# Hybrid mLSTM / attention block: the gate columns join the last v projection, and one v projection becomes 512 columns wide

## The chip, the cores and the metric

The kernel runs on one core of a Trainium2 chip. The metric is the device time of one launch in microseconds (us); lower is better. TensorE is called PE here, its weight loads PEld, VectorE DVE, ScalarE ACT, GpSimd POOL, and the queue that starts DMAs SP.

## What is computed

One layer of a decoder trunk with two token mixers side by side, on 512 tokens of width 1024, in fp32 (cut):

```python
h = rmsnorm(x, norm_g[l]) * (1.0 + scale[:, None]) + shift[:, None]
proj = h @ w_in[l]                       # 1024 -> 14344 columns
(qm, km, vm, om, zm, im, fm, qa, ka, va, za, gm, ga) = jnp.split(proj, split_idx, axis=-1)
...
im = im + b_if[l, :M_HEADS]              # input gate, 4 columns
fm = fm + b_if[l, M_HEADS:]              # forget gate, 4 columns
hm = mlstm_chunkwise(qm, km, vm, im, fm) # 4 heads
...
ha = diff_attention(qa, ka, va, lam, rel_bias)   # 8 heads, v of a head has 128 columns
ya = ha @ w_proj_a[l]
y = sigmoid(gm) * ym + sigmoid(ga) * ya
x = x + gate[:, None] * (y @ w_out[l])
return rmsnorm(x, final_g)
```

Of the 14344 columns only 8 are the gates `im` and `fm`; the attention's `va` has 1024, 256 for each pair of heads.

## The kernel before

Every fp32 product is made of three matmuls on split operands. A value is the sum of a rounded half `hi` and a rest `lo`, and `mm3` (lines 132 to 141) adds hi*hi, hi*lo and lo*hi into one PSUM bank. The normed input is held as `h_hi` and `h_lo` (8 blocks of 128 rows by 512 tokens) for the whole kernel.

Weights come in granules of 128x1024 fp32 (512 KB). `split_granule` (148 to 154) starts the DMA into a `raw` buffer, ACT casts it to `whi` (line 99) and DVE subtracts to get `wlo` (line 117). Each of the three has three buffers, so a granule's cast waits until PE is through with the granule three earlier. The table `_granules` (40 to 57) lays the columns of `w_in` out in the order of use: "F" granules hold q, k, v and z of the first pair of heads for one block of 128 rows; "B" 128 columns for all rows; "A" 256 columns for half of the rows; "W" 512 columns for a quarter of the rows.

The program runs in three parts.

1. **First pair** (lines 602 to 663). For each of 8 row blocks PE makes q, k, v and z of heads 0 and 1 while DVE and ACT still norm the input. Then `evac_qa`, `evac_ka`, `evac_v` and `silu2` empty the eight PSUM banks.
2. **Attention** (665 to 707). The heads are generators; `tick` (158) moves each one a step forward after every projection, so that their short matmuls lie between long projections. First `if_gates` (524 to 595) is started: it makes a granule of its own out of the 8 gate columns (a POOL memset, four DMAs, a cast, a subtraction), multiplies it in 16 matmuls (line 539), adds the bias, and in the steps after that works out log sigmoid, the running sum and maximum over the tokens, and writes two rows per head to `me_d` in DRAM; the mLSTM reads them back (lines 781, 782). Then for each pair `p` of 1 to 3: q, k, a merge gate, v (`proj_v`, 368 to 375, twice 4 row blocks), a merge gate, then the same q and k for the second head, and z. `proj_v` computes v with the tokens on the partitions: the stationary operand is a 128x128 block of h, the moving one 256 columns of weights, four token blocks in two banks.
3. **mLSTM, projections, output** (890 to 1013), four heads with `proj_w` (379 to 391) for v, 512 columns wide, one bank for each of the four token blocks.

PSUM has 8 banks: 4 of the pool `acc` for projections and 4 of `core` for the heads. A new tile takes the bank that was given up first. Each engine works through its queue in order; a scheduler sets that order when the program is built, from the order of the code and the priorities.

Of the kernel before, what the change touches and what calls it, by code (L numbers as in the profile page):

```python
# [9 lines left out]
F32 = mybir.dt.float32  # L10
# [53 lines left out]
@with_exitstack  # L64
def hybrid_block_kernel(ctx: ExitStack, tc: tile.TileContext, xT, x, c, wada2, wada, win, wif, wpm, wpa, wout,
                        small, lamv, bif, relb, onehot, fing, out):
# [75 lines left out]

    def load_granule(src):
        raw = stg.tile([P, D], F32, tag="raw", name=nm("raw"))
        nc.sync.dma_start(raw, src)
        return raw

    def split_granule(src):
        raw = load_granule(src)
        hi = stg.tile([P, D], F32R, tag="whi", name=nm("whi"))  # L150
        lo = stg.tile([P, D], F32R, tag="wlo", name=nm("wlo"))
        with tc.high_priority():
            split(hi, lo, raw, eng="act")
        return hi, lo
# [22 lines left out]
    lam4 = sb.tile([P, 384], F32, tag="bt", bufs=3, name="lam4")  # L177
    bift = const.tile([MH, 2], F32, name="bift")
    oneh = sb.tile([32, RL], F32, tag="bt", bufs=3, name="oneh")
# [49 lines left out]

    csl = sb.tile([P, D], F32, tag="v", bufs=2, name="csl")  # L230
    csl_done = []
# [127 lines left out]
    def evac_v(pss):  # L359
        v = sb.tile([P, 2, NT, 256], F32R, tag="v", bufs=2, name=nm("v"))  # L360
        vh, vl = v[:, 0], v[:, 1]
        for i in range(2):
            split(vh[:, 2 * i:2 * i + 2, :].rearrange("p a b -> p (a b)"),
                  vl[:, 2 * i:2 * i + 2, :].rearrange("p a b -> p (a b)"), pss[i])
        return vh, vl


    def proj_v(col, half, pss):
        hi, lo = split_granule(win[GIDX[("A", col, half)]])
        for kk in range(4):  # L370
            wsl = slice(kk * 256, kk * 256 + 256)
            mm_v(pss, half * 4 + kk, (hi[:, wsl], lo[:, wsl]))
        v = evac_v(pss) if half else None
        tick()
        return v

    def proj_w(col, quarter, pss, v):
        hi, lo = split_granule(win[GIDX[("W", col, quarter)]])  # L380
        for t in range(NT):
            for kk in range(2):
                k = quarter * 2 + kk
                tsl, wsl = slice(t * P, (t + 1) * P), slice(kk * S, (kk + 1) * S)
                mm3(pss[t], (h_hi[:, k, tsl], h_lo[:, k, tsl]), (hi[:, wsl], lo[:, wsl]), k == 0, k == NK - 1)
            if quarter == 3:
                if t % 2 == 0:
                    w = sb.tile([P, 2, 2, S], F32R, tag="v", bufs=2, name=nm("v"))
# [43 lines left out]
    ha = [None] * AH  # L432
    za = [None] * AH
    va = [None] * AH

    def hp_tiles():
# [5 lines left out]
    def attn_head(hd, q, k):  # L442
# [3 lines left out]
        bt = bias_tile(hd)  # L446
        vs = slice((hd % 2) * P, (hd % 2) * P + P)
        pt = sb.tile([P, 2, 1280], F32, tag="p", bufs=PB, name=nm("pt"))
# [46 lines left out]
        for kb in range(NT):  # L495
            c0 = min(kb, 2) * P
            a = slice(KOFF[kb], KOFF[kb] + S - c0)
            mm3(ps[:, c0:S], (va[hd][0][:, kb, vs], va[hd][1][:, kb, vs]), (ah[:, a], al[:, a]),
                kb == 0, kb == NT - 1, head=True)
# [22 lines left out]
    me_d = dram.tile([MH, 2 * S], F32, name="me_d")  # L522

    def if_gates():

        wraw = stg.tile([P, D], F32, tag="raw", name="wraw_if")
        nc.gpsimd.memset(wraw, 0.0)
        wr3 = wraw.rearrange("p (k n) -> p k n", n=P)
        for o in (0, 64):
            nc.sync.dma_start(wr3[:, :, o:o + MH], wif[:, :, MH:2 * MH])  # L530
            nc.sync.dma_start(wr3[:, :, o + 32:o + 32 + MH], wif[:, :, 0:MH])
        wih = stg.tile([P, D], F32R, tag="whi", name="wih")
        nc.scalar.copy(wih, wraw)
        wm = wih.rearrange("p (k n) -> p k n", n=P)
        nc.vector.tensor_tensor(wm[:, :, 64:128], wr3[:, :, 64:128], wm[:, :, 64:128].bitcast(F32), ALU.subtract)
        ps = acc_ps()
# [4 lines left out]
        g_i = sb.tile([P, S], F32, tag="z", bufs=8, name="g_i")[0:MH, :]  # L541
        g_p = sb.tile([P, S], F32, tag="z", bufs=8, name="g_p")[0:MH, :]
        for g, o, col in ((g_p, 0, 1), (g_i, 32, 0)):
            nc.scalar.activation(g, ps[o:o + MH, :], AF.Identity, bias=bift[:, col:col + 1])
            nc.vector.tensor_tensor(g, ps[o + 64:o + 64 + MH, :], g, ALU.add)
        yield
        for _ in range(2):
            yield

        ps = core_ps()  # L550
        for t in range(NT):
# [50 lines left out]
    for k in range(NK):  # L602
# [36 lines left out]
        if k == 1:  # L639
            nc.sync.dma_start(lam4[:, 0:256], lamv)  # L640
            nc.sync.dma_start(bift, bif)
        if k in (5, 6):
# [17 lines left out]
    q1, k1 = evac_qa(fq[1]), evac_ka(fk[1])  # L660
    va[0] = va[1] = evac_v(fv)
# [203 lines left out]
    def out_weights(k):  # L865
# [4 lines left out]
        elif k < 7:  # L870
            tag, bufs = {3: ("v", 2), 4: ("p", PB), 5: ("p", PB), 6: ("sw", 1)}[k]
            w2 = sb.tile([P, 2, D], F32R, tag=tag, bufs=bufs, name=nm("wo"))
# [17 lines left out]
    for h in range(MH):  # L890
# [11 lines left out]
        if h == 0:  # L902
            while None in ha:
                tick()
# [33 lines left out]

    gf = sb.tile([P, 2, D], F32, tag="v", bufs=2, name="gf")
    gate_b, fg = gf[:, 0, :], gf[:, 1, :]  # L940
# [143 lines left out]
```

## Time and profile before

| what | us |
|---|---|
| median of 3 runs | 925.57 (925.35 to 926.0) |
| profiled execution, own time | 924.88 |
| its span, first to last instruction | 923.1 |
| PE busy | 908.9 (98%) |
| DVE busy | 601.7 (65%) |
| ACT busy | 454.9 (49%) |
| POOL busy | 24.3 (3%) |

A matmul's busy time in the profile overlaps with the next one's, so a busy share of 98% does not say how much work PE has; the distance from one start to the next does. A row of the timeline gives start, duration, engine, line, operation, operands (partitions x elements) and a count; in square brackets how long the engine had been idle before it, and what released it.

### The profile page before, as it was taken

What the parts mean: (1) busy time and instruction counts of PE and PEld (TensorE: products, weight loads), DVE (VectorE), ACT (ScalarE), POOL (GpSimd) and SP (SyncE); (2) the same over time, 40 slices, a digit from 0 to 9 for tenths busy, and PEclk for the clock granted to TensorE, in tenths of its full rate; (3) what the DMA queues carried; (4) which work ended last, traced back from release to release, by engine and by line L of the source; (5) the groups of instructions that cost most, each with busy time, mean ns of one, the idle gap of its engine ahead of it and who ended that gap; (6) DMA issues with size and microseconds to landing.
All of it is one profiled execution on the core that took longest, in us unless ns stands there. A gap on an engine that the chain in (4) does not pass through costs nothing.

```text
span 923.1 us, 11500 instructions
## 1 busy us (share of the span) xinstructions
PE 908.9 (98%) x4351; PEld 762.5 (83%) x4351; DVE 601.7 (65%) x975; ACT 454.9 (49%) x741; POOL 24.3 (3%) x56
## 2 busy tenths in 40 slices
PE   6999999999999999999999999999999999999997
PEld 3888987988888888888888888888888888888886
DVE  7967788878666565435558544586554877638944
ACT  7546887766677554222354533454233553236422
POOL 0001010000001000000000000000000000000000
PEclk8999999999999999999999999999999999999999
DMA  9863414333422352432223223223132224336421
GB/s 343 336 186 119 131 65 138 126 137 126 149 84 100 117 169 100 151 137 89 87 76 111 93 72 93 89 96 110 69 114 69 92 99 152 137 114 223 142 80 57
DMA packets 40656, 114.90 MB, mean 124 GB/s; under 512 B 8289, under 2 KB 8553, under 8 KB 39578
## 3 DMA queue, kind: packets, MB, share of 16 engines
q1 hardware_dynamic: 40010, 113.11, 35.6%
q10 hardware_dynamic: 592, 1.07, 0.4%
q8 instruction: 34, 0.56, 0.2%
q14 instruction: 20, 0.16, 0.1%
HBM read 106.78 MB, written 10.00 MB: 127 GB/s over the span
## 4 chain that ended last, share of the span: by engine, by line
PE 92%; DVE 3%; DMA 2%; ACT 2%; issue 1%; SPq 0%; ACTq 0%
PE acc L134 26%; PE acc L135 26%; PE acc L136 26%; PE core L134 3%; PE core L135 3%; PE core L136 3%; PE core L459 1%; PE core L460 1%; PE core L489 1%; DVE wlo L117 1%; DMA relt<-in_relb_dram 1%; PE core L237 1%; DMA xt<-in_xT_dram 1%; ACT whi L99 0%; DMA ga<-gt_d 0%
## 5 line engine op out<-in xcount | busy, mean ns | idle before, releaser
L134 PE MATMUL acc<-h_hi,whi 128*128 128x512 f32 x688 | 269.1, 391 | 0.5 <-DVE qk L427 0.5
L117 DVE TENSOR_TENSOR wlo<-raw,whi 128x1024 fp32r<-128x1024 f32 x129 | 157.8, 1223 | 167.7 <-ACT whi L99 163.5
L99 ACT CAST whi<-raw 128x1024 fp32r<-128x1024 f32 x129 | 135.5, 1050 | 245.5 <-PE acc L135 175.9
L135 PE MATMUL acc<-h_lo,whi 128*128 128x512 f32 x656 | 255.8, 390 | 0.0
L136 PE MATMUL acc<-h_hi,wlo 128*128 128x512 f32 x656 | 255.5, 389 | 0.0
L134 PEld LDWEIGHTS acc<-h_hi,whi 128*128 128x128 f32 x688 | 129.4, 188 | 26.6 <-PE acc L539 0.8
L136 PEld LDWEIGHTS acc<-h_hi,wlo 128*128 128x128 f32 x656 | 123.2, 188 | 25.9
L135 PEld LDWEIGHTS acc<-h_lo,whi 128*128 128x128 f32 x656 | 123.3, 188 | 23.9
L134 PE MATMUL acc<-whi,h_hi 128*128 128x512 f32 (+1 forms) x224 | 77.1, 344 | 0.1
L136 PE MATMUL acc<-whi,h_lo 128*128 128x512 f32 (+1 forms) x224 | 77.0, 344 | 0.0
L135 PE MATMUL acc<-wlo,h_hi 128*128 128x512 f32 (+1 forms) x224 | 76.9, 343 | 0.0
L134 PE MATMUL acc<-hh,whi 128*128 128x512 f32 x192 | 74.7, 389 | 0.0
L135 PE MATMUL acc<-hl,whi 128*128 128x512 f32 x192 | 74.7, 389 | 0.0
L136 PE MATMUL acc<-hh,wlo 128*128 128x512 f32 x192 | 74.7, 389 | 0.0
L134 PEld LDWEIGHTS acc<-whi,h_hi 128*128 128x128 f32 x224 | 42.4, 189 | 5.5 <-ACT tmp L741 0.5
L135 PEld LDWEIGHTS acc<-wlo,h_hi 128*128 128x128 f32 x224 | 42.4, 189 | 5.0
L136 PEld LDWEIGHTS acc<-whi,h_lo 128*128 128x128 f32 x224 | 42.4, 189 | 5.0
L464 ACT ACTIVATE pt<-pt,mn 128x128 f32<-128x128 f32 (+3 forms) x64 | 35.5, 557 | 17.6 <-DVE mn L462 17.4
L136 PEld LDWEIGHTS acc<-hh,wlo 128*128 128x128 f32 x192 | 36.1, 188 | 7.5
L135 PEld LDWEIGHTS acc<-hl,whi 128*128 128x128 f32 x192 | 36.1, 188 | 7.4
L134 PEld LDWEIGHTS acc<-hh,whi 128*128 128x128 f32 x192 | 36.1, 188 | 7.4
L462 DVE CUSTOM_DVE_ANT_0 pt<-core,bt 128x128 f32<-128x128 f32 (+3 forms) x64 | 29.5, 486 | 14.7 <-PE core L460 14.3
(277 smaller groups left out, 1360.2 us busy)
## 6 DMA issues: line engine op xcount, KB each, us to landing
raw<-in_win_dram SPq DMA_DIRECT2D x112, 512.0 KB, 3.3
wa<-in_wada_dram SPq DMA_DIRECT2D x8, 1024.0 KB, 7.1
raw<-in_wpm_dram SPq DMA_DIRECT2D x16, 512.0 KB, 3.2
raw<-in_wada_dram SPq DMA_DIRECT2D x8, 512.0 KB, 3.2
raw<-in_wpa_dram SPq DMA_DIRECT2D x8, 512.0 KB, 3.4
raw<-in_wout_dram SPq DMA_DIRECT2D x8, 512.0 KB, 3.3
gt_d<-tmp SPq DMA_DIRECT2D x12, 256.0 KB, 2.2
toe_d<-rev_d SPq DMA_DIRECT2D x8, 320.0 KB, 6.2
```

Of the source, the lines that this page charges most:

```text
L99: recent["act"] = nc.scalar.copy(dst, src)
L117: recent["dve"] = nc.vector.tensor_tensor(lo, src, hi.bitcast(F32), ALU.subtract)
L134: a = nc.tensor.matmul(ps, lhs[0], rhs[0], start=start, stop=False)
L135: b = nc.tensor.matmul(ps, lhs[l[0]], rhs[l[1]], start=False, stop=False)
L136: c = nc.tensor.matmul(ps, lhs[r[0]], rhs[r[1]], start=False, stop=stop)
L237: a = nc.tensor.matmul(idle, ones_r, ones_w, start=True, stop=True)
L459: inorder(nc.tensor.matmul(ps, q[m][:, qs], kh[m][:, 0:wn], start=True, stop=False))
L460: inorder(nc.tensor.matmul(ps, q[m][:, qs], kl[m][:, 0:wn], start=False, stop=True))
L462: nc.vector.tensor_tensor_reduce(pp, ps[:, 0:w], bt[:, S - w:S], 1.0, BIG, ALU.add, ALU.min, mn[:, qb, m:m + 1])
L464: nc.scalar.activation(pp, pp, AF.Exp, scale=-1.0, bias=mn[:, qb, m:m + 1], accum_out=ls[:, qb, m:m + 1])
L489: inorder(nc.tensor.transpose(ps[:, n:n + P], pt[:, 0, o:o + P], ident))
```

## The change

The granule form "A" and `proj_v` are gone. v of pairs 1 and 2 is made in one `proj_w` of 512 columns, in pair 1's place; nothing stands in pair 2's place. v of pair 3 is made by a new `proj_g` from two granules of 128x1056 (`wvg`): 256 columns of v and the 8 gate columns side by side, 264 columns for each of four banks. The first part of `if_gates` (memset, DMAs, split, 16 matmuls, bias) is gone; the generator now starts after pair 3's `proj_g` and takes the gates from an SBUF tile `gates`, tokens on the partitions. So the forget gates need no transposition to begin with, and the input gates need four (new). The pool tag `v` has 3 buffers instead of 2, and the SBUF area kept for DMA descriptors shrinks from 8192 to 2048 bytes. The mLSTM's first head waits in the program text for `gates_done`.

```diff
     for p in range(1, 4):
         g += [("B", C_QA + 256 * p), ("B", C_KA + 256 * p)]
-        g += [("A", C_VA + 256 * p, 0), ("A", C_VA + 256 * p, 1)]
+        if p == 1:
+            g += [("W", C_VA + 256, i) for i in range(4)]
...
-    def proj_v(col, half, pss):
-        hi, lo = split_granule(win[GIDX[("A", col, half)]])
-        for kk in range(4):
-            wsl = slice(kk * 256, kk * 256 + 256)
-            mm_v(pss, half * 4 + kk, (hi[:, wsl], lo[:, wsl]))
-        v = evac_v(pss) if half else None
+    def proj_g(half, pss):
+        hi, lo = split_granule(wvg[half], 4 * VG)
+        if half:
+            w = sb.tile([P, 2, NT, 256], F32R, tag="v", bufs=VB, name=nm("v"))
+        for t in range(NT):
+            for kk in range(4):
+                k = half * 4 + kk
+                tsl, wsl = slice(t * P, (t + 1) * P), slice(kk * VG, (kk + 1) * VG)
+                mm3(pss[t][:, 0:VG], (h_hi[:, k, tsl], h_lo[:, k, tsl]), (hi[:, wsl], lo[:, wsl]), k == 0, k == NK - 1)
+            if half:
+                split(w[:, 0, t, :], w[:, 1, t, :], pss[t][:, 0:256])
+                nc.vector.tensor_tensor(gates[:, t, :], pss[t][:, 256:VG], bift, ALU.add)
         tick()
...
     def if_gates():
-        wraw = stg.tile([P, D], F32, tag="raw", name="wraw_if")
...
-        for k in range(NK):
-            for i, hx in enumerate((h_hi, h_lo)):
-                nc.tensor.matmul(ps, wih[:, k * P:(k + 1) * P], hx[:, k, :], start=(k == 0 and i == 0),
-                                 stop=(k == NK - 1 and i == 1))
...
-            pin(nc.tensor.transpose(ps[:, t * MH:(t + 1) * MH], g_p[:, t * P:(t + 1) * P], ident[0:MH, 0:MH]), "pe")
...
-        nc.vector.tensor_copy(f, ps[:, 0:NT * MH])
+        nc.vector.tensor_copy(f.rearrange("p (a b) -> p a b", b=MH), gates[:, :, MH:2 * MH])
...
         nc.scalar.copy(g_p, ps[0:MH, :])
         yield
+        ps = core_ps()
+        for t in range(NT):
+            pin(nc.tensor.transpose(ps[0:MH, t * P:(t + 1) * P], gates[:, t, 0:MH], ident), "pe")
+        nc.scalar.copy(g_i, ps[0:MH, :])
+        yield
...
-    gens.append(if_gates())
-    tick()
     gens.append(attn_head(0, q0, k0))
...
                 early_gate()
-                pss = [acc_ps(), acc_ps()]
-                proj_v(C_VA + 256 * p, 0, pss)
-                va[hd] = va[hd + 1] = proj_v(C_VA + 256 * p, 1, pss)
+                if p != 2:
+                    pss = [acc_ps() for _ in range(NT)]
+                if p == 1:
+                    v = []
+                    for quarter in range(4):
+                        proj_w(C_VA + 256, quarter, pss, v)
+                    va[2] = va[3] = va[4] = va[5] = v
+                if p == 3:
+                    proj_g(0, pss)
+                    va[6] = va[7] = [proj_g(1, pss)]
+                    gens.append(if_gates())
...
-            while None in ha:
+            while None in ha or not gates_done:
                 tick()
```

Three places show how the queues move. The first is ACT's queue at the seam between the first pair and the attention, before (`acc_200` to `acc_203` hold q and k of heads 0 and 1, `core_204` and `core_205` their v, `raw_669` and `raw_735` the first two granules of pair 1):

```order
L614 ACTIVATE h_hi<-xt_88,mod 128x512
L533 CAST wih<-wraw_if 128x1024
L99 CAST whi_671<-raw_669 128x1024
L413 ACTIVATE qk_578<-acc_200 64x512
L413 ACTIVATE qk_581<-acc_200 64x512
L425 CAST qk_584<-acc_202 64x512
L426 CAST qk_584<-acc_202 64x512
L99 CAST v_614<-core_204 128x512
```

and with the change (tile numbers are shifted: `raw_638` and `raw_704` are those granules, `acc_201` the first q bank, `core_205` the first v bank):

```order
L609 ACTIVATE h_hi<-xt_88,mod 128x512
L102 CAST whi_640<-raw_638 128x1024
L102 CAST whi_706<-raw_704 128x1024
L423 ACTIVATE qk_579<-acc_201 64x512
L102 CAST v_615<-core_205 128x512
L423 ACTIVATE qk_582<-acc_201 64x512
L435 CAST qk_585<-acc_203 64x512
L436 CAST qk_585<-acc_203 64x512
```

The gates' cast is gone, both granules are cast ahead of the emptying of the first q bank, and half a v bank now stands between the two halves of that emptying.

The second place is PE's queue at pair 1's v, before (`core_866` holds scores of head 1, `acc_871` two token blocks of v):

```order
L459 MATMUL core_866<-qk_608,qk_599 128x384
L460 MATMUL core_866<-qk_609,qk_599 128x384
L134 MATMUL acc_871<-whi_875,h_hi 128x256
L135 MATMUL acc_871<-wlo_876,h_hi 128x256
L136 MATMUL acc_871<-whi_875,h_lo 128x256
```

and with the change (`core_875` and `core_880` hold scores of head 1, `acc_833` is the third of four v banks):

```order
L471 MATMUL core_875<-qk_603,qk_597 128x512
L472 MATMUL core_875<-qk_604,qk_597 128x512
L471 MATMUL core_880<-qk_609,qk_600 128x512
L137 MATMUL acc_833<-whi_837,h_hi 128x512
L138 MATMUL acc_833<-wlo_838,h_hi 128x512
L139 MATMUL acc_833<-whi_837,h_lo 128x512
```

The matmuls are twice as wide, and the third v bank comes only after scores of head 1; it and the fourth are banks that q and k of head 2 had.

The third place is ACT's queue at the entry of the mLSTM, before (`acc_3106` is the first mLSTM q projection, `core_3093` the output gate's row):

```order
L715 ACTIVATE tmp_3096<-core_3093 8x128
L99 CAST whi_3241<-raw_3239 128x1024
L739 COPY tmp_3132<-acc_3106 128x512
L741 ACTIVATE tmp_3131<-acc_3106,sm 128x512
L746 ACTIVATE tmp_3138<-tmp_3131 128x512
L196 ACT_TABLE_LOAD
```

and with the change (`acc_2986` is that projection, `wt_3599` the first mLSTM head's decay matrix, made of `me_d` and `acol`):

```order
L716 ACTIVATE tmp_2976<-core_2973 8x128
L102 CAST whi_3127<-raw_3125 128x1024
L740 COPY tmp_3012<-acc_2986 128x512
L742 ACTIVATE tmp_3011<-acc_2986,sm 128x512
L790 ACTIVATE wt_3599<-wt_3599,acol 128x512
L790 ACTIVATE wt_3599<-wt_3599,acol 128x384
L790 ACTIVATE wt_3599<-wt_3599,acol 128x256 x2
L747 ACTIVATE tmp_3018<-tmp_3011 128x512
L199 ACT_TABLE_LOAD
```

The exponentials of the first mLSTM head (line 789 before, 790 now) stood some 30 us earlier among the last attention heads; now they stand ahead of the tanh of the first q projection.

## Rows read from the trace of the kernel before

**Rows 1.** The page, busy time of each engine over the span.

```profile
PE 908.9 (98%) x4351; PEld 762.5 (83%) x4351; DVE 601.7 (65%) x975; ACT 454.9 (49%) x741; POOL 24.3 (3%) x56
```

**Rows 2.** Busy time by stretch: first pair's projections, early attention, later attention.

```profile
core 0: us, PE busy (x) PEld busy (x) DVE busy (x) ACT busy (x) POOL busy (x), PEclk, DMA share, GB/s
...
22.00:66.20 44.20, 44.20 (x241) 38.43 (x240) 36.33 (x62) 20.38 (x28) 3.21 (x6) 1.00 0.77 266
...
120.00:150.00 30.00, 29.52 (x147) 24.22 (x146) 27.26 (x56) 25.90 (x48) 2.58 (x5) 1.00 0.34 107
150.00:200.00 50.00, 50.00 (x283) 43.97 (x282) 39.36 (x83) 35.57 (x65) 3.36 (x8) 1.00 0.40 137
```

**Rows 3.** PE timeline, gate matmuls (first and last of 16), then the next projection.

```profile
66.25 0.39 PE L539 MATMUL acc<-h_hi,wih 128*128 128x512 f32 x1
...
69.65 0.39 PE L539 MATMUL acc<-h_lo,wih 128*128 128x512 f32 x1
70.49 0.47 PE L134 MATMUL acc<-h_hi,whi 128*128 128x512 f32 x1 [0.45 <-DVE qk L427]
```

**Rows 4.** PE timeline: first of 4 score matmuls, first of 48 of v, the next.

```profile
91.11 0.33 PE L459 MATMUL core<-qk,qk 128*128 128x384 f32 x1
...
91.81 0.28 PE L134 MATMUL acc<-whi,h_hi 128*128 128x256 f32 x1
...
97.56 0.40 PE L459 MATMUL core<-qk,qk 128*128 128x512 f32 x1
```

**Rows 5.** PE timeline around a break in the attention, 142 to 146 us.

```profile
142.65 0.39 PE L136 MATMUL acc<-h_hi,wlo 128*128 128x512 f32 x1
143.16 0.41 PE L594 MATMUL core<-ident,g_i 4*128 4x4 f32 x4
...
144.30 0.39 PE L134 MATMUL acc<-h_hi,whi 128*128 128x512 f32 x1
145.04 1.31 PE L489 MATMUL core<-ident,pt 128*128 128x128 f32 x10 [0.36 <-DVE mn L462]
```

**Rows 6.** DVE timeline, the running sum of the gates; the weight split late in the attention.

```profile
129.51 1.21 DVE L583 TENSOR_TENSOR_SCAN g_F<-tmp,g_p 4x512 f32<-4x512 f32 x1
...
313.22 1.23 DVE L117 TENSOR_TENSOR wlo<-raw,whi 128x1024 fp32r<-128x1024 f32 x1 [3.52 <-ACT whi L99]
```

**Rows 7.** Timelines of ACT (three), DVE and PE at the seam, 60 to 66 us.

```profile
60.73 1.05 ACT L99 CAST whi<-raw 128x1024 fp32r<-128x1024 f32 x1 [4.49 <-PE core L135]
61.69 0.58 ACT L413 ACTIVATE qk<-acc 64x512 fp32r<-64x512 f32 x1
...
65.60 1.08 ACT L99 CAST v<-core 128x512 fp32r<-128x512 f32 x2
63.07 0.68 DVE L414 SCALAR_TENSOR_TENSOR qk<-acc,qk 64x512 fp32r<-64x512 f32 x1
64.03 0.28 PE L136 MATMUL core<-whi,h_lo 128*128 128x256 f32 x1
```

**Rows 8.** PE timeline, four transposes of the forget gates.

```profile
82.53 0.41 PE L552 MATMUL core<-ident,g_p 4*128 4x4 f32 x4
```

**Rows 9.** Timelines: SP's gate rows, POOL and ACT work on them, mLSTM entry, PE there.

```profile
137.79 0.28 SPq L587 DMA_DIRECT2D me_d<-g_p  x1
139.25 0.34 SPq L781 DMA_DIRECT2D mt<-me_d  x1
...
282.32 2.41 POOL L787 TENSOR_SCALAR_AFFINE_SELECT wt<-mt 128x512 f32<-128x512 f32 x4
296.48 2.02 ACT L789 ACTIVATE wt<-wt,acol 128x512 f32<-128x512 f32 x4
330.88 0.63 ACT L746 ACTIVATE tmp<-tmp 128x512 f32<-128x512 f32 x1 [2.44 <-issue]
336.26 0.95 PE L134 MATMUL acc<-whi,h_hi 128*128 128x512 f32 x2
```

**Rows 10.** DMA issues: the read of the gate rows, count, KB each, median us to landing.

```profile
mt<-me_d SPq DMA_DIRECT2D x4, 256.0 KB, 3.4
```

More of the change, by code (lines that the diff above doesn't have):

```diff
@@ L27 @@
 TB = 5
+VB = 3
+VG = 256 + 2 * MH
 M_SLOT = 7
@@ L64, in hybrid_block_kernel @@
 @with_exitstack
-def hybrid_block_kernel(ctx: ExitStack, tc: tile.TileContext, xT, x, c, wada2, wada, win, wif, wpm, wpa, wout,
+def hybrid_block_kernel(ctx: ExitStack, tc: tile.TileContext, xT, x, c, wada2, wada, win, wvg, wpm, wpa, wout,
                         small, lamv, bif, relb, onehot, fing, out):
@@ L141, in mm3, with load_granule, split_granule @@
             inorder(c)
-    def load_granule(src):
-        raw = stg.tile([P, D], F32, tag="raw", name=nm("raw"))
+    def load_granule(src, w=D):
+        raw = stg.tile([P, w], F32, tag="raw", name=nm("raw"))
         nc.sync.dma_start(raw, src)
         return raw
[L148 to L151, printed above, removed]
+    def split_granule(src, w=D):
+        raw = load_granule(src, w)
+        hi = stg.tile([P, w], F32R, tag="whi", name=nm("whi"))
+        lo = stg.tile([P, w], F32R, tag="wlo", name=nm("wlo"))
         with tc.high_priority():
@@ L177, in hybrid_block_kernel @@
     lam4 = sb.tile([P, 384], F32, tag="bt", bufs=3, name="lam4")
-    bift = const.tile([MH, 2], F32, name="bift")
+    bift = const.tile([P, 2 * MH], F32, name="bift")
     oneh = sb.tile([32, RL], F32, tag="bt", bufs=3, name="oneh")
@@ L226, in bias_tile @@
         return bt
-    csl = sb.tile([P, D], F32, tag="v", bufs=2, name="csl")
+    csl = sb.tile([P, D], F32, tag="v", bufs=VB, name="csl")
     csl_done = []
@@ L359, in evac_v @@
     def evac_v(pss):
-        v = sb.tile([P, 2, NT, 256], F32R, tag="v", bufs=2, name=nm("v"))
+        v = sb.tile([P, 2, NT, 256], F32R, tag="v", bufs=VB, name=nm("v"))
         vh, vl = v[:, 0], v[:, 1]
@@ L365, in evac_v @@
         return vh, vl
-    def proj_v(col, half, pss):
-        hi, lo = split_granule(win[GIDX[("A", col, half)]])
-        for kk in range(4):
-            wsl = slice(kk * 256, kk * 256 + 256)
-            mm_v(pss, half * 4 + kk, (hi[:, wsl], lo[:, wsl]))
-        v = evac_v(pss) if half else None
+    def proj_g(half, pss):
[10 more added lines that the diff above has]
+                nc.vector.tensor_tensor(gates[:, t, :], pss[t][:, 256:VG], bift, ALU.add)
         tick()
-        return v
+        return (w[:, 0], w[:, 1]) if half else None
     def proj_w(col, quarter, pss, v):
@@ L387, in proj_w @@
                 if t % 2 == 0:
-                    w = sb.tile([P, 2, 2, S], F32R, tag="v", bufs=2, name=nm("v"))
+                    w = sb.tile([P, 2, 2, S], F32R, tag="v", bufs=VB, name=nm("v"))
                     v.append((w[:, 0], w[:, 1]))
@@ L434, in hybrid_block_kernel @@
     va = [None] * AH
+    va_col = [0, P, 0, P, 2 * P, 3 * P, 0, P]
     def hp_tiles():
@@ L446, in attn_head @@
         bt = bias_tile(hd)
-        vs = slice((hd % 2) * P, (hd % 2) * P + P)
+        vs = slice(va_col[hd], va_col[hd] + P)
         pt = sb.tile([P, 2, 1280], F32, tag="p", bufs=PB, name=nm("pt"))
@@ L497, in attn_head @@
             a = slice(KOFF[kb], KOFF[kb] + S - c0)
-            mm3(ps[:, c0:S], (va[hd][0][:, kb, vs], va[hd][1][:, kb, vs]), (ah[:, a], al[:, a]),
+            mm3(ps[:, c0:S], [v_[:, kb % v_.shape[1], vs] for v_ in va[hd][kb * len(va[hd]) // NT]], (ah[:, a], al[:, a]),
                 kb == 0, kb == NT - 1, head=True)
@@ L522, in hybrid_block_kernel @@
     me_d = dram.tile([MH, 2 * S], F32, name="me_d")
+    gates = const.tile([P, NT, 2 * MH], F32, name="gates")
+    gates_done = []
     def if_gates():
-        wraw = stg.tile([P, D], F32, tag="raw", name="wraw_if")
[L527 to L536, printed above, removed]
-        for k in range(NK):
-            for i, hx in enumerate((h_hi, h_lo)):
-                nc.tensor.matmul(ps, wih[:, k * P:(k + 1) * P], hx[:, k, :], start=(k == 0 and i == 0),
-                                 stop=(k == NK - 1 and i == 1))
[L541 to L551, printed above, removed]
-            pin(nc.tensor.transpose(ps[:, t * MH:(t + 1) * MH], g_p[:, t * P:(t + 1) * P], ident[0:MH, 0:MH]), "pe")
         work = sb.tile([P, S], F32, tag="me", bufs=2, name="work")
         f, e, r, q = (work[:, 16 * i:16 * i + 16] for i in range(4))
-        nc.vector.tensor_copy(f, ps[:, 0:NT * MH])
+        nc.vector.tensor_copy(f.rearrange("p (a b) -> p a b", b=MH), gates[:, :, MH:2 * MH])
         yield
@@ L577, in if_gates @@
             pin(nc.tensor.transpose(ps[0:MH, t * P:(t + 1) * P], f[:, t * MH:(t + 1) * MH], ident), "pe")
+        g_i = sb.tile([P, S], F32, tag="z", bufs=8, name="g_i")[0:MH, :]
+        g_p = sb.tile([P, S], F32, tag="z", bufs=8, name="g_p")[0:MH, :]
         nc.scalar.copy(g_p, ps[0:MH, :])
+        yield
[3 more added lines that the diff above has]
+        nc.scalar.copy(g_i, ps[0:MH, :])
         yield
@@ L595, in if_gates @@
         nc.vector.tensor_copy(acol, ps[:, 0:NT * MH])
+        gates_done.append(True)
     fq = [acc_ps() for _ in range(2)]
@@ L640, in hybrid_block_kernel @@
             nc.sync.dma_start(lam4[:, 0:256], lamv)
-            nc.sync.dma_start(bift, bif)
+            nc.sync.dma_start(bift, bif.to_broadcast([P, 2 * MH]))
         if k in (5, 6):
@@ L660, in hybrid_block_kernel @@
     q1, k1 = evac_qa(fq[1]), evac_ka(fk[1])
-    va[0] = va[1] = evac_v(fv)
+    va[0] = va[1] = [evac_v(fv)]
     for i in range(2):
         za[i] = silu2(fz[i])
-    gens.append(if_gates())
-    tick()
     gens.append(attn_head(0, q0, k0))
@@ L870, in out_weights @@
         elif k < 7:
-            tag, bufs = {3: ("v", 2), 4: ("p", PB), 5: ("p", PB), 6: ("sw", 1)}[k]
+            tag, bufs = {3: ("v", VB), 4: ("p", PB), 5: ("p", PB), 6: ("sw", 1)}[k]
             w2 = sb.tile([P, 2, D], F32R, tag=tag, bufs=bufs, name=nm("wo"))
@@ L936, in hybrid_block_kernel @@
         pend = (h, hm)
-    gf = sb.tile([P, 2, D], F32, tag="v", bufs=2, name="gf")
+    gf = sb.tile([P, 2, D], F32, tag="v", bufs=VB, name="gf")
     gate_b, fg = gf[:, 0, :], gf[:, 1, :]
@@ L1061 @@
         "win": win,
-        "wif": wb[:, :, C_IF:C_IF + 8].transpose(1, 0, 2),
+        "wvg": np.concatenate([wb[:, :, C_VA + 768:C_VA + 1024], wb[:, :, C_IF:C_IF + 8]], axis=2)
+        .reshape(2, 4, P, VG).transpose(0, 2, 1, 3).reshape(2, P, 4 * VG),
         "wpm": a["w_proj_m"][0].reshape(4, 4, P, 4, 256).transpose(0, 3, 2, 1, 4).reshape(16, P, D),
@@ L1067 @@
         "lamv": np.broadcast_to(lamv[None, :], (P, 256)),
-        "bif": a["b_if"][0].reshape(2, MH).T,
+        "bif": a["b_if"][0].reshape(1, 2 * MH),
         "relb": a["rel_bias"],
@@ L1072 @@
     }
-    nc = _bacc.Bacc("TRN2", target_bir_lowering=False, num_devices=1, dynamic_dma_scratch_size=8192)
+    nc = _bacc.Bacc("TRN2", target_bir_lowering=False, num_devices=1, dynamic_dma_scratch_size=2048)
     arrays, args = {}, []
```

4 lines of the change are left out of this document (1 added, 3 removed).

## The prediction, made before the changed kernel was run

> **What bounds the kernel now.** I read the page's busy times first [rows 1]: PE 98%, DVE 65%, ACT 49%, DMA far below. A busy PE says little, since matmuls overlap in that count, so the next view is PE's timeline: is the step from one start to the next constant? It is. With 512 moving columns it is (69.65 - 66.25) / 15 = 0.227 us [rows 3], with 384 it is (91.81 - 91.11) / 4 = 0.175 us, with 256 it is (97.56 - 91.81) / 48 = 0.120 us [rows 4], and these three lie on one line of 0.42 ns per column and some 13 ns per matmul. Third, I searched the timeline for steps longer than that. From 22 us to the end, with a granted clock of 1.00 [rows 2], there are only three places with a break of 0.2 us or more: one of 0.61 us at 69.65 [rows 3], two of 0.28 and 0.51 us at 142.65 and 144.30 [rows 5], and one at 336.26, where two matmuls take 0.95 us in place of 0.227 + 0.39, so 0.33 us are lost [rows 9]. In the first pair's projections PE is busy for all of the 44.20 us [rows 2]. So PE's queue is the span, and work that leaves PE leaves the time, unless the engines around it then make PE wait.
>
> **The change part by part.** The sum is made against the profiled execution, 924.88 us, of which 923.1 are span; the rest, 1.8, stays.
>
> *The 16 gate matmuls go.* 16 x 0.227 = 3.63 us of PE [rows 3]. They hide nothing but the emptying of the first pair's banks, which is the next term. Their POOL memset, four DMAs, cast and subtraction ran while PE was full [rows 2] and are worth nothing.
>
> *The seam at 66.25 us.* Without them PE wants the first projection of pair 1 at 66.25, and its bank is the first q bank. By the order ACT casts the second granule first: 60.73 + 1.05 = 61.78; then the first half of the q bank, 0.58; DVE, after its own split of that granule, subtracts at 63.07 for 0.68, to 63.75. Next in ACT's queue is half a v bank, whose last matmul starts at 64.03 and takes 0.28, so it is cast from 64.35 to about 64.9 (1.08 for two); then the second q half, 0.58, to 65.5. DVE then has the v half and the q half, 0.65 and 0.68, and is done at 66.3 [rows 7]. Before, 0.15 us more went by between the release and PE's start (70.49 is 0.84 after 69.65, of which 0.45 are idle [rows 3]). So PE starts at some 66.45: a break of 0.2 in place of 0.61, a gain of 0.4. Ends: no break (gain 0.6), or one more ACT cast of 1.05 ahead of it (a loss of 0.6).
>
> *v, wider.* Before: 3 pairs x 96 = 288 matmuls of 256 columns, 288 x 0.120 = 34.5 us. After: 96 of 512 columns, 21.8 us, and 96 of 264, whose form no row shows; its price lies between the steps at 256 and 384, 0.120 and 0.175 [rows 4], and I take the line, 0.123, since it is nearest to 256: 11.8 us. Gain 0.9; with the upper end the three would be 38.6, a loss of 4.1. The rows say that the gain comes from the 13 ns that each of 96 vanished matmuls costs, less 768 new columns. The Trainium skill, TensorE: Matmul & The Clock Gate, section "Back-to-back issue gap", gives about N / 2.4 + 2.5 ns for an isolated matmul on a warm clock; by its 2.5 ns the 96 matmuls save 0.24 us and the 768 columns cost 0.32, so widening would lose 0.1 us; the steps above are 11 ns longer than the rule, and no run here shows 2.5.
>
> *Transposes.* Four of the forget gates go, 0.41 us [rows 8], four of the input gates come. Their form, 128 rows onto 4 columns, moves 128 columns; ten transposes of heads take 1.31 us with that many [rows 5], so some 0.1 each. I count a loss of 0.1 for all.
>
> *The gates' small work moves.* The log sigmoid, two scans of 1.21 us [rows 6] and two sums ran on DVE between 120 and 150 us, the tightest stretch: DVE 27.26 of 30 us, and the two breaks of rows 5 lie there, the second of them released by DVE [rows 2, 5]. With some 4 us less the share falls to 78%, that of the stretch from 150 to 200, 39.36 of 50, where PE has no break [rows 2]. So I take the 0.8 as gained; ends 0 and 0.8. In its new place, at the end of the attention, DVE is idle half of the time: before the split at 313.22 it waited 3.52 us [rows 6].
>
> *New waits.* The 512-wide v takes all four banks of its pool. The third and fourth are given up only when q and k of head 2 are emptied, behind scores of head 1 on both engines. Following ACT's and DVE's order from the seam with the durations of the trace, the third bank comes 0.3 us late and the fourth in time; ends 0 and 1.2 (two more ACT steps of 0.58 [rows 7]). After that pair 2 has no v: PE loses 11.5 us of cover there, DVE only some 3.5 us of splits (two of 1.23, two of about 0.6). If a pair's stage took 67 us at 79% DVE, it becomes (52.9 - 3.5) / 55.5 = 89%; at the 91% of 120 to 150 us the breaks were 0.8 us in 30 [rows 2, 5], so 0 to 1.5. I take 0.3.
>
> *Entry of the mLSTM.* ACT's four exponentials, 2.02 us, now stand ahead of the tanh at 330.88. ACT waited 2.44 us there, for DVE's convolution, so they fit [rows 9], if their input is there at 328.4. I put the scan behind the split at 313.22 [rows 6]: with the second scan and the splits in between, the row of maxima is ready near 319; 1.5 us from write to read (137.79 to 139.25 [rows 9]), held some 0.2 by the exponential of the other row, 3.4 for the read [rows 10], 2.41 on POOL [rows 9]: 326.5, with 1.9 us to spare. Cost 0, the 0.33 stays; ends -0.3 and +0.5.
>
> Sum: -3.6 - 0.4 - 0.9 + 0.1 - 0.8 + 0.3 + 0.3 = **-5.0 us**, so 919.9 for the profiled execution. The median of the runs is 0.7 above the profiled one, so a median of 920.6.
>
> **The rivals.** A difference of over 0.2% (1.85 us) is about what a measurement of this kernel can tell from none.
>
> *The cover is missed.* The seam, the v banks and pair 2 all sit at their upper ends: 1.0 + 0.9 + 1.2 more, 923.7 at most. For it: DVE at 91% made breaks [rows 2, 5]. Against: each break so far was below 0.65 us. 921.8 to 923.7.
>
> *Columns alone count.* If a matmul had no fixed cost, v would lose 768 columns x 0.42 ns = 0.3 in place of gaining 0.9: 921.8. The steps at 256, 384 and 512 speak against it [rows 4, 3]. This is where the rule of the skill named above leads.
>
> *264 columns run like 384.* 96 x (0.175 - 0.123) = 5.0 us more: 925.6, no change. The three steps on one line speak against it.
>
> *ACT stands still at the mLSTM's entry, and it gets slower.* ACT works in order. If the row of maxima or its read comes late, ACT waits at the exponentials, and behind it stand the tanh, a weight cast and the copy of the k projection whose bank PE waits for at 336.26 [rows 9]. The first 2.3 us of lateness are free (1.9 and the 0.4 that the exponentials leave of the 2.44), each one after that costs 1. It takes 2.3 + 5.0 + 1.85 = 9.2 us to be slower than before; with 12 us late the time is 930.3. For it: a serial chain through five engines and DRAM, placed at its latest moment. Against: the read takes 3.4 us [rows 10], and SP issues it ahead of the six reads of merge gates.
>
> **How the numbers follow.** The forecast, with its own range of 918.9 to 921.8, gets 0.72; the missed cover 0.13, of which 0.02 above 923.7; columns alone 0.04; 264 as 384 0.04; the standing ACT or another such wait 0.07, of which 0.06 slower by over 0.2%. So faster 0.87, same 0.07, slower 0.06. The low end is every break gone, including that at 336.26: 0.2 + 0.6 + 0.33 under the forecast, 919.5, less 0.6 for the spread of the runs (925.35 to 926.0). The high end takes in most of the missed cover: 923.2. Some 0.15 lies outside, most of it above.
>
> **What would show it.** No instruction with the form 128x256 in a v projection, 96 with 128x264 at a step near 0.123 us, PE's count down by 106 rows of the queue. At the seam the first projection of pair 1 follows the last one of the first pair by less than 0.7 us, without a wait for the second granule. No break near the first scores of head 3. The exponentials of the first mLSTM head lie between the convolution's copies and the tanh, and PE's break there is of 0.0 to 0.8 us. I am wrong if PE's timeline shows breaks that add up to over 3 us after 66 us, if the step at 264 is above 0.14, or if the total of PE's steps falls by less than 4 us.

## The result, and the profile after

The changed kernel is **slower**, by 1.3%: 937.0 us median against 925.55, a ratio of 1.0128 (95% interval 1.0116 to 1.0140). All ratios here compare executions at a granted clock of 0.99 or more; one execution of run 7 below, 1298.4 us at 0.656, is not among them. 920.6 with a range of 918.9 to 923.2 had been forecast. The profiled execution has a span of 935.6 us against 923.1, so 12.5 us more, where 5.0 less were expected.

The page answers to [rows 1]:

```profile
span 935.6 us, 11268 instructions
PE 921.7 (99%) x4239; PEld 756.2 (81%) x4239; DVE 600.3 (64%) x978; ACT 453.4 (48%) x741; POOL 24.3 (3%) x55
```

PE has 112 instructions fewer and is busy 12.8 us longer. A new wait would have left PE idle; what grew is the work itself. The groups by line and form show which work (line, operation, form, count | busy, mean ns of one | idle before). First the kernel before, then after:

```profile
L134 PE MATMUL acc<-h_hi,whi 128*128 128x512 f32 x688 | 269.1, 391 | 0.5 <-DVE qk L427 0.5
L135 PE MATMUL acc<-h_lo,whi 128*128 128x512 f32 x656 | 255.8, 390 | 0.0
L136 PE MATMUL acc<-h_hi,wlo 128*128 128x512 f32 x656 | 255.5, 389 | 0.0
```

```profile
L137 PE MATMUL acc<-h_hi,whi 128*128 128x512 f32 x688 | 270.6, 393 | 0.5 <-DVE gates L383 0.4
L139 PE MATMUL acc<-h_hi,wlo 128*128 128x512 f32 x656 | 260.5, 397 | 0.0
L138 PE MATMUL acc<-h_lo,whi 128*128 128x512 f32 x656 | 259.8, 396 | 0.0
```

The code, the operands and the counts are the same, and in two of the three groups one matmul takes 6 to 8 ns longer. Of 0.39 us some 0.16 overlap with the next matmul, so the view that decides is the timeline. It is shown here at 385 us, in the mLSTM, a stretch that the change does not touch, where the heads' outputs `hh`, `hl` are projected. Before:

```profile
384.90 0.39 PE L134 MATMUL acc<-hh,whi 128*128 128x512 f32 x1
385.12 0.39 PE L135 MATMUL acc<-hl,whi 128*128 128x512 f32 x1
385.35 0.39 PE L136 MATMUL acc<-hh,wlo 128*128 128x512 f32 x1
...
386.94 0.39 PE L134 MATMUL acc<-hh,whi 128*128 128x512 f32 x1
```

After:

```profile
385.47 0.39 PE L137 MATMUL acc<-hh,whi 128*128 128x512 f32 x1
385.69 0.40 PE L138 MATMUL acc<-hl,whi 128*128 128x512 f32 x1
385.92 0.40 PE L139 MATMUL acc<-hh,wlo 128*128 128x512 f32 x1
...
387.55 0.39 PE L137 MATMUL acc<-hh,whi 128*128 128x512 f32 x1
```

Nine matmuls of 512 columns take 386.94 - 384.90 = 2.04 us before, 0.227 each, and 387.55 - 385.47 = 2.08 after, 0.231 each. No idle time stands in any row. It is not the clock either. In the stretch from 340 to 420 us, in which nearly every matmul has 512 columns, the count of PE's matmuls falls from 354 to 346 at a granted clock of 1.00 in both (PE busy, count, clock, DMA share, GB/s), before and then after:

```profile
340.00:420.00 80.00, 80.00 (x354) 1.00 0.38 132
```

```profile
340.00:420.00 80.00, 80.00 (x346) 1.00 0.37 125
```

Over the whole trace from 22 us on, the mean step of a 512-column matmul is 0.2276 us before (3409 of them) and 0.2320 after (3485, steps above 0.33 us left out): 3485 x 0.0044 = **15.3 us**. With the 16 gate matmuls (-3.6), v (34.5 before, 288 at a mean of 0.1198; 96 x 0.2276 + 96 x 0.121 = 33.5 at the old step, -1.0) and the breaks (4.5 before, 6.4 after, +1.9; a step counts as a break where it is 0.05 us or more above its form's usual one, with what it is above) that makes 12.6, against 12.5 measured.

What could lengthen a matmul whose code is untouched? One difference of the built programs touches all of them, the places of the tiles in SBUF. The changed kernel's `split_granule` is also called with 4 x 264 = 1056 columns, and all buffers of a tile name in a pool have the size of the largest, so each of the three buffers of `raw`, `whi` and `wlo` grew from 4096 to 4224 bytes per partition, 128 more. These are the first bytes of the tiles in the built programs (no view of the profile shows them), and in brackets what is left of them after division by 256:

```
              before                                  after
h_hi, h_lo    10784 (32)  27168 (32)                  4640 (32)   21024 (32)
whi           56096 (32)  60192 (32)  64288 (32)      50464 (32)  54688 (160)  58912 (32)
wlo           68384 (32)  72480 (32)  76576 (32)      63136 (160) 67360 (32)   71584 (160)
hh, hl        all 32                                  all 32
```

Before, every operand of a long projection begins at 32 within 256 bytes. After, of each granule's two halves one begins 128 bytes off. Sorted by the buffers, the steps of products with the normed input are 0.2274 us before (2479 of 512 columns), and after 0.2316 where lo is off (some 1700) and 0.2326 where hi is off (some 860). That is a correlation; the runs had to show whether it is the cause.

### The profile page after: what moved, and what is told of

Its sections match the earlier page's. It is cut to its first block, busy times and chain, and to the rows that moved or that the text cites. A ratio compares the mean times of both kernels' runs of the same rounds, so it can differ in the third digit from the quotient of the medians.

```text
span 935.6 us, 11268 instructions
## 1 busy us (share of the span) xinstructions
PE 921.7 (99%) x4239; PEld 756.2 (81%) x4239; DVE 600.3 (64%) x978; ACT 453.4 (48%) x741; POOL 24.3 (3%) x55
## 4 chain that ended last, share of the span: by engine, by line
PE 94%; ACT 2%; DVE 2%; DMA 1%; issue 1%; SPq 0%; ACTq 0%
PE acc L138 26%; PE acc L139 26%; PE acc L137 26%; PE core L138 4%; PE core L139 4%; PE core L137 4%; PE core L471 1%; PE core L472 1%; PE core L501 1%; DMA relt<-in_relb_dram 1%; PE core L240 1%; DMA xt<-in_xT_dram 1%; ACT L199 0%; PE core L333 0%; ACT whi L102 0%
## 5 line engine op out<-in xcount | busy, mean ns | idle before, releaser
L139 PE MATMUL acc<-h_hi,wlo 128*128 128x512 f32 x656 | 260.5, 397 | 0.0
L138 PE MATMUL acc<-h_lo,whi 128*128 128x512 f32 x656 | 259.8, 396 | 0.0
L137 PE MATMUL acc<-whi,h_hi 128*128 128x512 f32 (+1 forms) x192 | 72.5, 378 | 0.0
L138 PE MATMUL acc<-wlo,h_hi 128*128 128x512 f32 (+1 forms) x192 | 72.0, 375 | 0.0
L139 PE MATMUL acc<-whi,h_lo 128*128 128x512 f32 (+1 forms) x192 | 71.8, 374 | 0.0
L137 PEld LDWEIGHTS acc<-whi,h_hi 128*128 128x128 f32 x192 | 36.1, 188 | 7.6 <-DVE qk L437 0.4
L139 PEld LDWEIGHTS acc<-whi,h_lo 128*128 128x128 f32 x192 | 36.0, 188 | 7.2
L138 PEld LDWEIGHTS acc<-wlo,h_hi 128*128 128x128 f32 x192 | 36.1, 188 | 6.4
```

Of the source, the lines that this page charges most:

```text
L137: a = nc.tensor.matmul(ps, lhs[0], rhs[0], start=start, stop=False)
L138: b = nc.tensor.matmul(ps, lhs[l[0]], rhs[l[1]], start=False, stop=False)
L139: c = nc.tensor.matmul(ps, lhs[r[0]], rhs[r[1]], start=False, stop=stop)
```

## The experiments

**Theory.** The step of a 512-column matmul depends on where its two operands begin within 256 bytes. **Rival, load:** the longer steps come of something else in the change, wider transfers, a third v buffer, less room for descriptors, other neighbours in time. The first four runs tell them apart: the change with its placement mended, and the kernel before with the placement broken. In all four each engine runs the same instructions in the same order as the kernel that they start from. The kernel before ran beside them at 924.76 us (924.79 beside the later ones); ratios are to that.

**Run 1, the change with the halves 4352 bytes apart** (17 x 256; all six begin at 32):

```diff
-        hi = stg.tile([P, w], F32R, tag="whi", name=nm("whi"))
-        lo = stg.tile([P, w], F32R, tag="wlo", name=nm("wlo"))
+        hi = stg.tile([P, 1088], F32R, tag="whi", name=nm("whi"))[:, 0:w]
+        lo = stg.tile([P, 1088], F32R, tag="wlo", name=nm("wlo"))[:, 0:w]
```

> The changed kernel with nothing but the buffers of the two weight halves made 4352 bytes apart (1088 columns, of which the granule uses the first 1024 or 1056) in place of 4224, so that all six begin at the same offset within 256 bytes as the normed input does. Placement theory: the step of a 512-column matmul, 0.2320 us on average in the changed kernel and 0.2276 before, depends on where its two operands begin within 256 bytes; 3485 of them fall back by 0.0044 us each, 15.3 us, and the time becomes 937.0 - 15.3 = 921.7 us, faster than before by some 0.4%. Rival, load: the longer steps come from the other things that the change brings (rows of 4224 bytes in two transfers, a third v buffer, the smaller area for DMA descriptors, other neighbours in time); these stay, and so do 0.232 and 937 us.

Measured: 922.74 us, a ratio of 0.9983 (0.9974 to 0.9992). The mean step is back at 0.2279, the matmuls from 340 to 420 us are 356, and the same groups read:

```profile
L137 PE MATMUL acc<-h_hi,whi 128*128 128x512 f32 x688 | 269.1, 391 | 0.5 <-DVE gates L383 0.4
L138 PE MATMUL acc<-h_lo,whi 128*128 128x512 f32 x656 | 256.0, 390 | 0.0
L139 PE MATMUL acc<-h_hi,wlo 128*128 128x512 f32 x656 | 255.8, 390 | 0.0
```

32 columns more per buffer, which nothing reads, take 13.5 us away (from +11.5 to -2.0 against the kernel before). Wider transfers, v buffers and descriptor area are as in the change; the load rival falls. The one microsecond over the 921.7 is in part the breaks, which add up to 7.1 us here and 6.4 in the changed kernel, and in part the step, which is 0.2 ns longer than in the kernel before (3484 of them, 0.8 us). That the breaks grow because a faster PE leaves less slack under the other engines is an explanation that was not tried.

**Run 2, the kernel before with the halves 4224 bytes apart**, nothing else of the change in it:

```diff
-        hi = stg.tile([P, D], F32R, tag="whi", name=nm("whi"))
-        lo = stg.tile([P, D], F32R, tag="wlo", name=nm("wlo"))
+        hi = stg.tile([P, 1056], F32R, tag="whi", name=nm("whi"))[:, 0:D]
+        lo = stg.tile([P, 1056], F32R, tag="wlo", name=nm("wlo"))[:, 0:D]
```

> The kernel before, order and arithmetic as they were, with the buffers of the two weight halves 4224 bytes apart in place of 4096: hi at 32, 160, 32 and lo at 160, 32, 160 bytes within 256, the normed input at 32, as in the changed kernel. Placement theory: 3409 matmuls of 512 columns go from 0.2276 to 0.232 us, 15 us, and the time from 925.55 to some 940.5 us. Rival, load: nothing of the change is in here, so 925.5 us and 0.2276.

Measured: 934.57 us, 1.0116 (1.0100 to 1.0131); mean step 0.2307. The placement alone makes the kernel slower, but by 10 us and not by 15. The reason can be read from the buffers: here the gates' own granule takes a buffer of hi and none of lo, so from then on hi and lo are out of turn by one. With 32, 160, 32 for hi and 160, 32, 160 for lo, a third of the granules then have both halves at 32, a third one of them, and a third none. Sorted by pairs, with the normed input at 32:

```
hi at  lo at   matmuls   mean step, ns
  32     32       779        227.9
  32    160       892        231.2
 160    160       764        232.6
```

In the changed kernel, without that granule, no pair is whole. So the size of the effect is a matter of which buffers meet. In the kernel's total, 3409 steps that are 3.1 ns longer make 10.4 us, and 9.8 were measured.

**Run 3, the kernel before with 128 bytes more between the normed input and the weights:**

```diff
-    acol = const.tile([P, NT * MH], F32, name="acol")
+    acol = const.tile([P, NT * MH + 32], F32, name="acol")[:, 0:NT * MH]
```

> The kernel before with one tile that lies between the normed input and the weight buffers made 128 bytes longer: all weight halves, and all tiles behind them (the heads' outputs too), begin at 160 bytes within 256, and the normed input stays at 32. Placement theory, first form (what counts is the moving operand against the stationary one): each product with the normed input, some 2500 matmuls of 512 columns, goes from 0.227 to 0.233 us, 14 us, to some 939 us; the projections of the heads' outputs (both operands at 160) stay at 0.227. Second form (what counts is that the stationary operands of neighbours differ among themselves): no change, 925.5. Rival, load: 925.5.

Measured: 938.26 us, 1.0151 (1.0137 to 1.0165), as the first form says. Both kinds of product are in one trace. Normed input at 32 against weights at 160 (ten steps, the first rows and the last):

```profile
353.71 0.40 PE L135 MATMUL acc<-wlo,h_hi 128*128 128x512 f32 x1
353.95 0.39 PE L136 MATMUL acc<-whi,h_lo 128*128 128x512 f32 x1
354.18 0.39 PE L134 MATMUL acc<-whi,h_hi 128*128 128x512 f32 x1
...
356.04 0.39 PE L136 MATMUL acc<-whi,h_lo 128*128 128x512 f32 x1
```

and 32 us later the heads' outputs at 160 against weights at 160 (twelve steps):

```profile
385.62 0.39 PE L136 MATMUL acc<-hh,wlo 128*128 128x512 f32 x1
385.85 0.39 PE L134 MATMUL acc<-hh,whi 128*128 128x512 f32 x1
...
388.34 0.39 PE L136 MATMUL acc<-hh,wlo 128*128 128x512 f32 x1
```

(356.04 - 353.71) / 10 = 0.233 us and (388.34 - 385.62) / 12 = 0.227 us. All weight halves lie alike here, so that they differ among themselves is not what costs; the distance between moving and stationary operand is. The narrow v projection of pair 1, whose operands are as far apart, pays nothing: 48 matmuls of 256 columns from 91.20 to 96.89 us, 0.119 each, against the 0.120 of [rows 4].

```profile
91.20 0.28 PE L134 MATMUL acc<-whi,h_hi 128*128 128x256 f32 x1
...
96.89 0.40 PE L459 MATMUL core<-qk,qk 128*128 128x512 f32 x1
```

**Run 4, the kernel before with the halves 4128 bytes apart** (as in run 2, 1032 columns), for other distances:

> The kernel before with the buffers of the weight halves 4128 bytes apart: hi at 32, 64, 96 and lo at 128, 160, 192 bytes within 256, the heads' tiles at 224, the normed input at 32. One look, for the step as a function of the distance between the two operands. Placement theory, if only the distance within 256 bytes counts: steps of 0.227 for the first granule buffer's hi after hi alone, longer ones for the rest, about 0.233, a time of 938 to 945 us; if it counts within 64 bytes or less, the buffers at 32, 96 and 160 stay at 0.227 and those at 64, 128 and 192 rise. Rival, load: 925.5 us.

Measured, one run: 938.44 us, mean step 0.2321. Steps by the buffers of a granule, the normed input at 32: 231.6 ns for 32 and 160 (779 matmuls), 232.5 for 64 and 192 (764), 231.6 for 96 and 128 (786). So no granule with such distances, 32 to 160 bytes, is free, and none is much worse than another. The time and the mean step are as the first half of the expectation has them; step by step it is mixed, 229.0 ns for hi after hi in the first buffer, 228.3 to 234.6 for the other sequences with the normed input. So a single step between two unequal places can be almost free, and why is open; the mean over a granule never was. The second half, a period of 64 bytes or less, falls: hi at 96, 64 bytes from the normed input, has the 234.6. Distances of whole 256 bytes are free, whether or not they are whole 512: before, the weights stand at 288 within 512 and the normed input at 32.

With the placement out of the way, the aligned change gains 2.0 us and not 5. The next runs divide it in its two halves.

**Run 5, the gates' half alone** (halves 4352 apart):

```diff
-        if p == 1:
-            g += [("W", C_VA + 256, i) for i in range(4)]
+        if p < 3:
+            g += [("A", C_VA + 256 * p, 0), ("A", C_VA + 256 * p, 1)]
...
-                if p == 1:
-                    v = []
-                    for quarter in range(4):
-                        proj_w(C_VA + 256, quarter, pss, v)
-                    va[2] = va[3] = va[4] = va[5] = v
+                if p < 3:
+                    proj_v(C_VA + 256 * p, 0, pss)
+                    va[hd] = va[hd + 1] = [proj_v(C_VA + 256 * p, 1, pss)]
```

> The gates' half of the change alone, with the weight halves 4352 bytes apart: pairs 1 and 2 take their v 256 columns wide, each in its own place, as before; pair 3's v has the gate columns beside it. Theory (the terms of the prediction hold for the gates, and the breaks that the widened v brings ate the rest): 16 matmuls less, 3.6 us; the seam 0.3; the matmuls of 264 columns at 0.121, nothing; against before some -3.5 to -4.3 us, and of the breaks that the changed kernel has at the first scores after the seam, at two places of pair 2 and at pair 3's v only the last stays. Rival (the breaks come from the gates' new place and from the order as such): they stay, and with the 1.4 us that 288 narrow matmuls cost over the wide ones the time is 0 to -0.6 us against before.

**Run 6, the wide v alone** (the kernel before, the granules of pair 1 and the loop over pairs as in the change, pair 3 as before, `if_gates` untouched):

```diff
-        g += [("A", C_VA + 256 * p, 0), ("A", C_VA + 256 * p, 1)]
+        if p == 1:
+            g += [("W", C_VA + 256, i) for i in range(4)]
+        if p == 3:
+            g += [("A", C_VA + 256 * p, 0), ("A", C_VA + 256 * p, 1)]
```

> The other half alone: the kernel before, gates in their own 16 matmuls, v of pairs 1 and 2 in one projection of 512 columns in pair 1's place, pair 3's v 256 wide; three v buffers and the small descriptor area, both needed for the space; weight halves 4096 apart. Theory: v itself saves 192 x 0.121 - 96 x 0.2279 = 1.35 us, pair 2 without v and the wait for the banks cost about 1.5 to 2.5 us of breaks, so 0 to +1.2 us against before. Rival (as predicted, breaks of 0.6): -0.7 us, and -3.8 of the gates explain all that the aligned kernel gains.

Measured: the gates alone 921.34 us, 0.9967 (0.9955 to 0.9979), by the medians -3.5 us; the wide v alone 926.13, 1.0012 (1.0003 to 1.0021), by the medians +1.3. Together -2.1, and run 1 had -2.0: the halves add up. Run 5 is at the near end of what was expected of it, run 6 just above its own 0 to +1.2. **Run 5 is faster than both kernels**, and the widening is a loss. The breaks tell why (their sum: 4.7 us in run 5, 7.1 in run 6, 4.5 before): in run 6 the steps of v save 192 x 0.1198 - 96 x 0.2278 = 1.1 us, and the breaks cost 2.6 more. Two in run 6 are in pair 2, which has no v of its own there:

```profile
210.99 0.49 PE L493 MATMUL core<-ident,pt 128*128 128x128 f32 x3
211.89 0.55 PE L493 MATMUL core<-ident,pt 128*128 128x128 f32 x3 [0.41 <-DVE pt L479]
...
239.98 0.39 PE L138 MATMUL acc<-h_lo,whi 128*128 128x512 f32 x1
240.66 0.33 PE L493 MATMUL core<-ident,pt 128*128 128x128 f32 x1 [0.30 <-DVE pt L479]
```

PE comes to the transposes of a head before DVE has normalized the rows (line 479): 0.57 and 0.46 us lost. Run 1 has the same two, run 5 neither. A third stands at 143.66, where 0.97 us of idle time await the same line. Run 5 in its turn has two that run 6 lacks:

```profile
72.11 0.40 PE L137 MATMUL acc<-h_hi,whi 128*128 128x512 f32 x1
72.90 0.39 PE L480 MATMUL core<-qk,qk 128*128 128x256 f32 x1 [0.40 <-DVE z L419]
...
255.86 0.39 PE L481 MATMUL core<-qk,qk 128*128 128x512 f32 x1
256.63 0.47 PE L137 MATMUL acc<-h_hi,whi 128*128 128x512 f32 x1 [0.39 <-DVE gates L392]
```

The first is the seam's: without 3.6 us of gate matmuls PE wants a bank for the first scores while DVE still empties z out of it. That it stays in run 5 had not been expected. The second is the gate addition's, which is now the last reader of the v bank that the next projection waits for.

**Run 7, run 1 with everything 224 bytes further**, the operands at 0 within 256 instead of 32:

```diff
+    const.tile([P, 56], F32, name="shift")
     h_hi = const.tile([P, NK, S], F32R, name="h_hi")
```

> The changed kernel with the weight halves 4352 bytes apart and the normed input, the weight halves and all behind them moved by 224 bytes, so that they begin at 0 within 256 bytes and not at 32. Placement theory, only the distance between the operands counts: 0.2279 per matmul of 512 columns and 922.7 us, as without the move. Rival (the place itself counts, and operands that begin at a multiple of 64 bytes are read faster): steps below 0.222 us, 20 us less.

Measured: 923.76 us, 0.9990 (0.9980 to 1.0000), mean step 0.2279 as in run 1. That median is over all ten executions, the ratio as said above. Operands at 0 run like operands at 32; the 13 ns per matmul beyond the columns do not go away with a start at a multiple of 256.

## Why the prediction was wrong

**The step that failed** is the first one: "is the step from one start to the next constant? It is", read as a price that belongs to the width alone. From it came "work that leaves PE leaves the time". The 3400 matmuls that the change does not touch were thereby costed at nothing, without work that hides it or a reason. They cost 15.3 us, which is the difference between -5.0 and +12.5 but for 2.2, and that is in the main the breaks. All three steps were measured in one program, with one placement; that a granule of 4 x 264 columns makes the buffers of both halves 128 bytes longer could be read from the diff. The rival for "slower" had the wrong mechanism, and the range could not hold the result.

**Point by point**, with the placement taken out:

- *The 16 gate matmuls*, -3.6: right. Run 5 gains 3.5 us with them, its breaks being 0.3 more than before.
- *264 columns*, 0.123 predicted, 0.121 measured: the second 48 stand together, 47 steps from 254.17 to 259.86. The rival "264 like 384" fell. After:

```profile
254.17 0.28 PE L137 MATMUL acc<-whi,h_hi 128*128 128x264 f32 x1
...
259.86 0.29 PE L139 MATMUL acc<-whi,h_lo 128*128 128x264 f32 x1
```

- *v, wider*, -0.9 predicted, -1.0 by the steps of an aligned kernel. But as time it is +1.3 (run 6, which leaves the gate columns out): the term was right, and the waits that it brings were taken too small. By the Trainium skill, TensorE: Matmul & The Clock Gate, section "Back-to-back issue gap", this term would lose 0.1 (an estimate from its 2.5 ns for an isolated matmul); the steps measured here, 0.227, 0.121 and 0.120 us, decide against it. The loss of run 6 does not bear it out either, since there it is the breaks that lose.
- *The seam*, a break of 0.2 predicted, -0.4: the break at 67.04 is 0.29. The text stopped there, and the wait only moved on to the first scores at 74.63 (0.43): together 0.1 worse than the 0.61 of before (0.2 worse in runs 1 and 5). Rows after:

```profile
67.04 0.40 PE L139 MATMUL core<-h_hi,wlo 128*128 128x512 f32 x1
67.56 0.47 PE L137 MATMUL acc<-h_hi,whi 128*128 128x512 f32 x1
...
74.63 0.40 PE L137 MATMUL acc<-h_hi,whi 128*128 128x512 f32 x1
75.29 0.39 PE L471 MATMUL core<-qk,qk 128*128 128x256 f32 x1 [0.26 <-DVE z L410]
```

- *The v banks*, 0.3: the third 0.25 and the fourth 0.29 late, 0.5 in all, where the fourth was to be in time. After:

```profile
92.44 0.40 PE L471 MATMUL core<-qk,qk 128*128 128x512 f32 x1
92.80 0.50 PE L137 MATMUL acc<-whi,h_hi 128*128 128x512 f32 x1
...
95.70 0.40 PE L139 MATMUL acc<-whi,h_lo 128*128 128x512 f32 x1
96.10 0.50 PE L137 MATMUL acc<-whi,h_hi 128*128 128x512 f32 x1
```

- *Pair 2 without v*, 0.3: 0.44 at 208.15 and 0.25 at 237.18, and 0.5 each in run 1, so about 0.7 to 1.0. The mechanism was named (DVE's share rises where PE loses cover); the size was not.
- *The gates' scans off DVE*, -0.8: of the breaks at 142 to 146 us 0.16 is left at 140.12, but 0.45 in run 1 and 0.67 in run 5. Run 6, which keeps the scans where they were, has 1.10 at 142.49. They were put down to the scans; a part does go with these, but a head's transposes that wait for its normalization stay.
- *The gate addition as last reader of a bank*: a term that the sum does not have. 0.53 lost, on PE 0.37 of it idle. After:

```profile
260.68 0.39 PE L472 MATMUL core<-qk,qk 128*128 128x512 f32 x1
261.44 0.47 PE L137 MATMUL acc<-h_hi,whi 128*128 128x512 f32 x1 [0.37 <-DVE gates L383]
```

- *The mLSTM's entry*, 0, and the rival in which ACT stands still: the exponentials came without a wait in front of them, 329.58 us, directly behind ACT's copies, and the tanh followed at 332.13. The break of 0.33 at 336.26 [rows 9] is gone, a gain of 0.3 that had not been counted; in run 6, whose gates are early as before, a break of that size stands at 337.58.

```profile
328.90 0.78 ACT L742 ACTIVATE tmp<-acc,sm 128x512 f32<-128x512 f32 x1
329.58 2.02 ACT L790 ACTIVATE wt<-wt,acol 128x512 f32<-128x512 f32 x4
332.13 0.63 ACT L747 ACTIVATE tmp<-tmp 128x512 f32<-128x512 f32 x1 [0.53 <-ACT wt L790]
```

Two counts of the prediction are off without weight. Its list of breaks lacks one of 0.25 us at 113.73, between a head's transposes and the next scores, which every run has. And PE's count fell by 112 (16 gate matmuls and 96 of v), not by 106.

In all, the breaks were to fall by 0.6 us (-0.4, -0.8 and twice +0.3) and rose by 1.9. So even with the placement mended the forecast of -5.0 would have been too high: run 1 has -2.0, as in "the cover is missed" (921.8 to 923.7, or -3.8 to -1.9), a rival that had 0.13. The number falls in that rival's stretch, and its mechanism is in part what runs 1 and 6 show: breaks at the seam, at the v banks and in pair 2.

## What to carry to other kernels

When an edit changes the size of a pooled tile, the other buffers of that pool move, and with them the operands of code that it does not touch: compare the tiles' first bytes in the two built programs before taking a step from the old trace, and keep moving and stationary operands of matmuls with 512 columns a multiple of 256 bytes apart (here 1088 columns for granules of 1024 and 1056). When PE is full, work that is taken away or moved forward can uncover what lay under it; follow the queue past the first wait to the next one, and ask of each new small reader whether it is the last to hold a bank. And halves of a change are to be timed one by one: here one gained 3.5 us and the other lost 1.3.

## What had not been expected of the hardware

- On the fp32 operands of this kernel, a 512-column matmul starts its successor after 0.227 us when both operands begin at the same place within 256 bytes and, in the mean of a granule with a half elsewhere, after 0.231 to 0.233 (distances of 32, 64, 96, 128 and 160 bytes; single sequences in run 4 from 0.228 to 0.235); with 256 columns no difference was seen (0.119 at a distance of 128). That the distance is the cause is shown by runs 1 to 3. Why PE or SBUF needs the time stays open; no run here looks inside a step.
- It counts for the weights of the matmul that runs and for those of the next one. In the changed kernel, where the normed input or a head's output moves, the step is 0.2276 us with both sets at the moving operand's place, 0.2330 where only the next one is off, 0.2335 where only the running one is and 0.2336 where both are (some 600, 850, 830 and 310 matmuls). Where the weights move, as in `proj_w`, the steps do not sort so simply (0.2287 to 0.2354 by sequence).
- The place itself made no difference where it was tried: operands at 0 within 256 bytes run like those at 32 (run 7), and at 160 like both (run 3).
- Even with equal places some steps of 0.230 to 0.236 us are left (10% of the 512-column steps before, none from 340 to 420 us). They stand mostly in twos; what they hang on was not tried.
